# A hybrid attention and state-space layer: large loads on GpSimd's queue and later, combining weights a step later, the last gate loaded early, the output weight's split on GpSimd

## The chip, the cores and the metric

The kernel runs on one core of a Trainium2 chip. The metric is the device time of one execution in microseconds (us); the median of several executions is compared. A core has a matrix engine (TensorE, PE in the profile; PEld is its weight load), VectorE (DVE), ScalarE (ACT), GpSimd (POOL) and SyncE (SP), each with its own instruction stream that is worked off in order. DMA transfers are issued here by SyncE or by GpSimd.

## The reference

```python
proj = jnp.einsum('bsd,de->bse', x, w_in[layer])
q, k, v, z_att, z_ssm, xbc, dt_raw = jnp.split(proj, list(SPLITS), axis=-1)
o1, l1 = dilated_window_attention(q, k, v, slopes, 1)     # 16 heads of 64, window 128 steps
o2, l2 = dilated_window_attention(q, k, v, slopes, 4)
o3, l3 = dilated_window_attention(q, k, v, slopes, 16)
wts = jax.nn.softmax(jnp.stack([l1, l2, l3], axis=0), axis=0)
y_att = wts[0][..., None] * o1 + wts[1][..., None] * o2 + wts[2][..., None] * o3
y_att = rms_norm(y_att.reshape(Bsz, S, D_ATT) * jax.nn.silu(z_att), att_norm_g[layer])
xbc = jax.nn.silu(causal_depthwise_conv(xbc, conv_w[layer], conv_b[layer]))
...
y = ssd_chunked(xs_h, dt, a, bm, cm)                       # Mamba-2 scan, chunks of 128
y = y + d_skip[layer][:, None] * xs_h
y_ssm = rms_norm(y.reshape(Bsz, S, D_SSM) * jax.nn.silu(z_ssm), ssm_norm_g[layer])
mix = jnp.concatenate([y_att, y_ssm], axis=-1)
x = layer_norm(alpha * x + jnp.einsum('bse,ed->bsd', mix, w_out[layer]), ln_g[layer], ln_b[layer])
```

One sequence of 2048 positions, model width 1024, attention and state-space parts of 1024 columns each; all float32. The three outputs of a head are combined by a softmax over their log-sum-exps.

## The kernel before, in words

Matmul operands are split into a high and a low float32r part, and three products stand for one (high times high, high times low, low times high).

**Projections, convolution, scan (up to about 1270 us).** x is loaded transposed and split; v, then the convolution columns, then the state-space gate `z_ssm` (`ez`, L310), then q, k and the attention gate are projected, and the chunked scan (`ssd`) is woven between the last of these. Results go to DRAM tensors: d_qh, d_ql, d_kh, d_kl (high and low parts of q and k for each pair of heads), d_v (v in the block order of each of the three dilations), d_za (the attention gate), d_us (the state-space branch), d_uh (its first four row blocks, split already). In the z_ssm stage `split_w` also loads the output weight `wout` in halves of 512 columns (`woraw`), scales and rounds the high part (`wot`, L326), has VectorE form the low part (L327) and stores both to d_wo. In these stages a scheduler orders the instructions, on SyncE in the later ones too.

**Attention (about 1270 to 1830 us).** Here the order on TensorE, VectorE, ScalarE and GpSimd is that of the program. The list `todo` runs over 8 pairs of heads, 3 dilations d, 4 groups of blocks qd and 2 halves: a half-unit (d, qd, half) is two blocks of 128 queries for two heads. Step i of the loop does `scores` of half-unit i (matmuls S, L528; bias and row minimum on VectorE, L536; exponential on ScalarE, L544), `transposes` of half-unit i-2 (T, L557, evacuated by VectorE, L559) and `values` of half-unit i-3 (N, L577, into `num`). Most of the rest of the loop's body, including the places named (d, qd, half), goes by the half-unit whose `values` were just done. For each pair:

- `load_pair` and `load_qk` fetch the next pair's kh, kl, qh, ql (1 MB each, L462, GpSimd's queue), at (0,3,0); kh and kl have two buffers, qh and ql one.
- `load_dil` fetches a dilation's bias table `tb` and its v (1 MB, L472, SyncE's queue): for the next pair at (0,3,1) and (1,3,1), for dilation 2 of this pair at (0,3,1). v has three buffers.
- `permute` reorders qh and ql for dilations 1 and 2 into `qp` on GpSimd (L492, L496).
- `statistics` transposes the row minima and sums on TensorE (L595), copies them on ScalarE (L597, `sT`) and writes them to d_st with small SyncE DMAs (L599 to L605): after dilation 1, and after dilation 2 at the end of the pair. `gather` reads them back into `cm` in another layout (L611).
- `weights` of the pair before forms the softmax over dilations: part 0 (L618 to L621, VectorE and ScalarE) at (0,2,1), part 1 (L624 to L628, then the store to d_wd, L629) at (0,3,0).
- `combine` of the pair before, in four steps at (0,3,0), (1,0,0), (1,2,0), (2,2,0), on GpSimd: three times load the weights spread over partitions (`wb`, 1 MB, L642, SyncE), multiply `num` (L644) and add (L653); the fourth loads the gate (L657), multiplies (L659) and stores the branch to d_ua (L660).

In the last pair the loads of the output weight W from d_wo (`load_w`, L675, 1 MB each) and of d_uh (`fetch_parts`, L689) take the place of the next pair's loads, in buffers that have become free (`big`, `ring`).

**Output product (about 1830 us to the end).** For 16 blocks of 128 rows, `product` multiplies a branch (1 is state-space, 0 attention) by its half of W: 48 matmuls (L737 to L739) in two halves of 24, with a small matmul (L743) between the halves that sums the squares (`squares`, L712 and L714, on the branch's raw rows from `fetch_raw`) for the norm. `residual` loads x (L718); `add` applies the norm (L750, L755), `norm` is the layer norm. The branch 1 products of four row blocks come first, while pair 7 is finished: its gate is multiplied into `num` (L841, two on GpSimd, one on VectorE), then come `weights`, `combine` on VectorE, and the rest of W.

Of the kernel before, what the change touches and what calls it, by code (L numbers as in the profile page):

```python
# [9 lines left out]
F32 = mybir.dt.float32  # L10
# [8 lines left out]
NR = 16  # L19
# [9 lines left out]
def hybrid_layer(ctx, tc, xT, xc, w52, wv, convw, convb, dtb, alog, dskp, gcol, wout,  # L29
# [46 lines left out]
    with ExitStack() as c1:  # L76
# [178 lines left out]
        with tc.tile_pool(name="dtp", bufs=1, reuse_waits="tile") as dp, \  # L255
# [63 lines left out]
            def split_w(e):  # L319
                g = gc[:, e:e + 1]  # L320
                for hf in range(2):
                    s = slice(hf * 512, hf * 512 + 512)
                    raw = wo.tile([128, 512], F32, name="woraw")
                    nc.sync.dma_start(raw, wout[e * 128:(e + 1) * 128, s])
                    t = wo.tile([128, 2, 512], F32R, name="wot")
                    nc.scalar.activation(t[:, 0], raw, AF.Copy, scale=g)  # L326
                    nc.vector.scalar_tensor_tensor(t[:, 1], raw, g, t[:, 0].bitcast(F32), op0=OP.mult,  # L327
                                                   op1=OP.subtract)
                    nc.sync.dma_start(d_wo[e][:, :, s], t.bitcast(F32))
# [109 lines left out]
    with ExitStack() as c2:  # L439
# [11 lines left out]
        def load_pair(pr):  # L451

            A = {"pr": pr, "num": [], "tab": {}, "v": {}, "q": {0: []}, "k": []}
            load_qk(A, "k", d_kh, d_kl, qk[pr % 2])
            A["st"] = stp.tile([128, 192], F32, name="st")
            return A

        def load_qk(A, x, dh, dl, pool):
            to = A["q"][0] if x == "q" else A["k"]
            for src, n in ((dh, "h"), (dl, "l")):  # L460
                t = pool.tile([128, NR, NJ], F32R, name=x + n, bufs=1)
                nc.gpsimd.dma_start(f2(t), src[A["pr"]])  # L462
                to.append(t)

        def load_dil(A, d):

            pr = A["pr"]
            tb = A["tab"][d] = io.tile([128, 2, (128, 256, 256)[d]], F32, name=f"tb{d}", bufs=1)
            c0 = (512, 256, 0)[d]
            nc.sync.dma_start(tb, tabs[2 * pr:2 * pr + 2, :, c0:c0 + tb.shape[2]].rearrange("h p c -> p h c"))  # L470
            v = A["v"][d] = io.tile([128, 16, 128], F32, name="v", bufs=3)
            nc.sync.dma_start(v, d_v[d][:, :, pr * 128:pr * 128 + 128].rearrange("b p e -> p b e"))  # L472
# [219 lines left out]
        def fetch_raw(n, br):  # L692
            u = raw[n, br] = row().rearrange("p (c t) -> p c t", t=128)
            if br:
                for g in range(2):
                    nc.sync.dma_start(u[:, 4 * g:4 * g + 4], d_us[g][n])
            else:
                nc.sync.dma_start(u[:, 0:7], d_ua[n])
# [17 lines left out]
        def residual(n):  # L716
            o = O[n] = os_[n // 2][:, n % 2 * D:n % 2 * D + D] if n < 4 else O.pop(n - 4)
            nc.sync.dma_start(o, xc[n * 128:(n + 1) * 128, :])  # L718
# [3 lines left out]
        UT = ["num", "num", "num"]  # L722
# [56 lines left out]

        O = {}  # L780
# [5 lines left out]
        with tc.manual_schedule(engines={E.PE, E.DVE, E.Activation, E.Pool}):  # L786
            for i in range(len(todo) + TA + 1):
                if i < len(todo):
                    pr, d, qd, half = todo[i]
                    if i == 0:  # L790
                        pairs[0] = load_pair(0)
                        load_qk(pairs[0], "q", d_qh, d_ql, io)
# [11 lines left out]
                if i > TA:  # L804
# [4 lines left out]
                    if (d, qd, half) == (2, 3, 1):  # L809
                        statistics(pairs[pr], 1)  # L810
                        gather(pairs[pr])
                    if pr < 7:
                        if (d, qd, half) == (0, 3, 0):
                            pairs[pr + 1] = load_pair(pr + 1)
                            load_qk(pairs[pr + 1], "q", d_qh, d_ql, io)
                        if (qd, half) == (3, 1) and d < 2:
                            load_dil(pairs[pr + 1], d)
                    elif (d, qd, half) == (0, 3, 0):
                        for e, name in ((8, "kh_0"), (9, "kl_0"), (10, "qh"), (11, "ql")):
                            load_w(e, name)  # L820
                    elif (d, qd, half) == (1, 2, 0):
                        for e, name in ((12, "v"), (13, "qp"), (14, "qp")):
                            load_w(e, name)
                    elif (d, qd, half) == (1, 3, 1):
                        load_w(15, "v")
                    elif (d, qd, half) == (2, 1, 0):
                        for n in range(3):
                            fetch_parts(n, 1)
                    if pr and (d, qd, half) == (0, 3, 1):
                        load_dil(pairs[pr], 2)  # L830
                    if pr and d == 0 and (qd, half) in ((2, 1), (3, 0)):
                        weights(pairs[pr - 1], qd - 2)
                    step = ((0, 3, 0), (1, 0, 0), (1, 2, 0), (2, 2, 0))
                    if pr and (d, qd, half) in step:
                        combine(pairs[pr - 1], step.index((d, qd, half)))
            A = pairs[7]
            small = stp.tile([128, 192], F32, name="st")
            zt = cm_.tile([128, NR, NJ], F32, name="wb", bufs=3)
            nc.sync.dma_start(f2(zt), d_za[7])
            for d in range(3):  # L840
                (nc.vector if d == 2 else nc.gpsimd).tensor_tensor(A["num"][d], A["num"][d], zt, op=OP.mult)  # L841
            for n in range(3):
                fetch_raw(n, 1)
            os_ += [big("kh_1", F32), big("kl_1", F32)]
            for e, name in ((0, "qp"), (1, "qp"), (2, "v")):
                load_w(e, name)
            order = [(n, 1) for n in range(4)] + [(n, 0) for n in range(4)]
            order += [(n, br) for n in range(4, 16) for br in (1, 0)]
            squares(0, 1)
            residual(0)  # L850
            for i, (n, br) in enumerate(order):
                ps = product(n, br)
                if i == 0:
                    weights(A, 0)
                    residual(1)
                    weights(A, 1)
                if i == 1:
# [6 lines left out]
                    for e, name in ((3, "num"), (4, "num"), (5, "num"), (6, "wb"), (7, "wb")):  # L864
# [89 lines left out]
```

## Time and profile before

| | |
|---|---|
| median of 3 runs | 2244.34 us (2242.55 to 2248.68) |
| profiled execution | 2245.68 us, span 2243.9 us, mean TensorE clock 0.974 |
| busy | TensorE 2145.6 us, VectorE 1155.1, ScalarE 866.7, GpSimd 759.6 |
| DMA | 363.66 MB, 162 GB/s on the mean; SyncE's queue 306.76 MB, GpSimd's 54.53 MB |
| stage 1295 to 1835 us (attention) | TensorE busy 495.6 of 540 us, DMA share 0.68 |
| stage 1835 to 1900 us (first products) | TensorE busy 31.9 of 65 us, DMA share 0.89 |

How to read the lines. A row of the waits is: engine, tile and line that waited, the engine, tile and line that released it, us in total, times, longest. A row of the timeline is: start, duration, engine, line, operation, output and inputs, shape, count, and in brackets the idle time of that engine before it with what ended it. A row of a table by stretches is: the stretch, its length, then busy time and instructions of TensorE, its weight load, VectorE, ScalarE, GpSimd, then the granted clock, the DMA share and GB/s. A row of the chain of work that ended last is: start, duration, engine or DMA, tile.

### The profile page before, as it was taken

The numbers are of one execution on the slowest core, as the hardware profiler recorded it, in microseconds if no ns is written. First come the engines' busy times: TensorE is split into PE (matmuls) and PEld (weight loads), VectorE is DVE, ScalarE is ACT, GpSimd is POOL, SyncE is SP. The second block draws the span as 40 slices with busy tenths as digits, with TensorE's granted clock in tenths as the row PEclk, the third lists the DMA queues.
The fourth block names the chain that finished last, engine by engine and source line by source line (L and its number), as shares of the span: only waits on it lengthen the run. The fifth ranks groups of instructions, "written<-read, shape, count | busy, mean of one in ns | idle before, by whom it ended". The sixth has DMA issues, their size and how long they took to land.

```text
span 2243.9 us, 37059 instructions
## 1 busy us (share of the span) xinstructions
PE 2145.6 (96%) x13968; PEld 1789.4 (80%) x13968; DVE 1155.1 (51%) x2940; ACT 866.7 (39%) x2321; POOL 759.6 (34%) x527
## 2 busy tenths in 40 slices
PE   8999999999999999999999999899988976999998
PEld 8999888888778888888888788677776755888886
DVE  4000265553203555444644278777877756665655
ACT  4101122224322332232355378677776741222221
POOL 3101011010012555555654314456644562232322
PEclk9999999999999999999999889999999997999999
DMA  8544222226865565555543637767587698222220
GB/s 287 168 136 134 80 66 76 70 81 201 282 188 195 199 216 186 177 181 176 188 139 111 228 92 217 203 196 205 138 229 203 182 291 273 90 101 99 76 94 32
DMA packets 257219, 363.66 MB, mean 162 GB/s; under 512 B 37776, under 2 KB 175120, under 8 KB 246800
## 3 DMA queue, kind: packets, MB, share of 16 engines
q1 hardware_dynamic: 247952, 306.76, 44.9%
q0 software_dynamic: 9088, 54.53, 6.6%
q8 instruction: 110, 1.80, 0.3%
q14 instruction: 69, 0.57, 0.1%
HBM read 226.62 MB, written 134.61 MB: 161 GB/s over the span
## 4 chain that ended last, share of the span: by engine, by line
PE 80%; DMA 11%; DVE 3%; SPq 2%; issue 2%; ACT 2%; POOL 1%; ACTq 0%; DVEq 0%; POOLq 0%
PE pp L113 12%; PE pp L111 12%; PE pp L112 12%; PE S L528 6%; PE N L577 6%; PE T L557 6%; PE S L737 3%; PE S L739 3%; PE S L738 3%; DMA woraw<-wout 3%; DMA d_st<-sT 3%; PE pp L155 2%; PE pp L156 2%; PE pp L154 2%; PE T L737 2%
## 5 line engine op out<-in xcount | busy, mean ns | idle before, releaser
L111 PE MATMUL pp<-xh,whi 128*128 128x512 f32 x1408 | 550.8, 391 | 4.8 <-ACT ez L310 4.8
L112 PE MATMUL pp<-xl,whi 128*128 128x512 f32 x1408 | 549.5, 390 | 0.0
L113 PE MATMUL pp<-xh,wlo 128*128 128x512 f32 x1408 | 548.7, 390 | 0.0
L544 ACT ACTIVATE P<-P,st 128x256 f32<-128x256 f32 (+1 forms) x768 | 345.1, 451 | 97.2 <-DVE st L536 97.1
L111 PEld LDWEIGHTS pp<-xh,whi 128*128 128x128 f32 x1408 | 264.3, 188 | 61.1 <-ACT ez L310 6.7
L113 PEld LDWEIGHTS pp<-xh,wlo 128*128 128x128 f32 x1408 | 264.3, 188 | 55.1
L112 PEld LDWEIGHTS pp<-xl,whi 128*128 128x128 f32 x1408 | 264.4, 188 | 54.2
L536 DVE CUSTOM_DVE_ANT_0 P<-S,tb 128x256 f32<-128x256 f32 (+1 forms) x768 | 235.2, 362 | 105.8 <-PE S L528 48.6
L101 POOL TENSOR_TENSOR wlo<-wraw,whi 128x1024 fp32r<-128x1024 f32 x44 | 105.4, 2396 | 496.6 <-ACT whi L100 496.6
L577 PE MATMUL N<-PT,v 128*64 128x128 f32 x2400 | 179.4, 287 | 41.8 <-DVE PT L559 41.8
L559 DVE COPY PT<-T 128x512 f32<-128x512 f32 (+1 forms) x304 | 196.5, 677 | 2.3 <-PE T L557 2.2
L577 PEld LDWEIGHTS N<-PT,v 128*64 128x64 f32 x2400 | 131.3, 140 | 76.2 <-DVE PT L559 43.4
L557 PE MATMUL T<-ident,P 128*128 128x128 f32 x1200 | 180.0, 288 | 0.8 <-ACT P L544 0.3
L644 POOL TENSOR_TENSOR wb<-num,wb 128x2048 f32<-128x2048 f32 x21 | 96.2, 4580 | 171.3 <-DMA wb<-d_wd 101.2
L557 PEld LDWEIGHTS T<-ident,P 128*128 128x128 f32 x1200 | 131.7, 144 | 24.4 <-ACT P L544 1.8
L544 ACT ACTIVATION_READ_ACCUMULATOR P<-P,st 128x1 f32 x768 | 143.9, 187 | 0.0
L528 PE MATMUL S<-kh,qp 64*128 64x256 f32 (+1 forms) x1024 | 130.3, 313 | 0.0
L379 DVE TENSOR_SCALAR mt<-csb,cs 128x128 f32<-128x128 f32 x256 | 73.5, 357 | 74.3 <-DMA csb<-d_cs 66.1
L528 PEld LDWEIGHTS S<-kh,qp 64*128 64x128 f32 x1024 | 91.7, 194 | 23.0 <-issue 22.0
L154 PE MATMUL pp<-vh,xh 128*128 128x384 f32 (+1 forms) x304 | 95.1, 321 | 5.9 <-ACT xh L184 5.3
L128 DVE SCALAR_TENSOR_TENSOR ev<-pp,ev 128x512 f32<-128x512 f32 x64 | 44.0, 687 | 106.2 <-ACT ev L127 105.4
L714 DVE TENSOR_REDUCE tb<-P 128x128 f32<-128x1024 f32 x32 | 63.9, 1998 | 66.3 <-PE N L743 48.9
(288 smaller groups left out, 3737.9 us busy)
## 6 DMA issues: line engine op xcount, KB each, us to landing
v<-d_v SPq DMA_DIRECT2D x24, 1024.0 KB
wb<-d_wd SPq DMA_DIRECT2D x48, 512.0 KB
wraw<-w SPq DMA_DIRECT2D x44, 512.0 KB
d_wo<-wot SPq DMA_DIRECT2D x32, 512.0 KB
csb<-d_cs SPq DMA_DIRECT2D x32, 512.0 KB
d_v<-vt SPq DMA_DIRECT2D x64, 192.0 KB
d_za<-ev SPq DMA_DIRECT2D x32, 256.0 KB
d_xs<-cvo SPq DMA_DIRECT2D x8, 1024.0 KB
```

Of the source, the lines that this page charges most:

```text
L101: nc.gpsimd.tensor_tensor(lo, raw, hi.bitcast(F32), op=OP.subtract)
L111: nc.tensor.matmul(ps, hi[:, k, :], h, start=(k == 0), stop=False)
L112: nc.tensor.matmul(ps, hi[:, k, :], l, start=False, stop=False)
L113: nc.tensor.matmul(ps, lo[:, k, :], h, start=False, stop=(k == 7))
L154: nc.tensor.matmul(ps, h, vw[k][0], start=(k == 0), stop=False)
L528: nc.tensor.matmul(ov(sp[h][:, 256 * b:256 * b + w]), A["q"][d][x][hr, blk], kv(A["k"][y][hr]), start=(m == 0), stop=(m == 2))
L536: nc.vector.tensor_tensor_reduce(P[:, h, b, 256 - w:256], sp[h][:, c0:c0 + w], tab[:, h, tab.shape[2] - w:], 1.0, 3.0e38, OP.add, OP.min, ...
L544: nc.scalar.activation(p, p, AF.Exp, bias=stat(A, 0, d, h, blk), scale=-1.0, accum_out=stat(A, 1, d, h, blk))
L557: nc.tensor.transpose(tp[:, h, b], P[:, h, b, 128 * which:128 * which + 128], ident)
L559: nc.vector.tensor_copy(pt[:, :, bl[0]:2], tp[:, :, bl[0]:2])
L577: nc.tensor.matmul(nm[64 * h:64 * h + 64, bq * 128:bq * 128 + 128], v[:, k, 64 * h:64 * h + 64], pts[which][:, h, b], start=(f or not whic ...
L737: nc.tensor.matmul(ps, uh[:, e, :], wh, start=(e == 0), stop=False)
```

## The change

- `split_w`: the high part of the output weight is formed on GpSimd instead of ScalarE.
- `load_qk`: the next pair's four loads are issued together, in the order qh, kh, ql, kl, at (1,0,0), behind `combine` step 0; before, kh, kl, qh, ql at (0,3,0).
- `load_dil`: v is issued on GpSimd's queue, in program order; `tb` stays on SyncE.
- `weights` parts 0 and 1 go to (0,3,0) and (0,3,1); `combine` steps to (1,0,0), (1,1,0), (1,3,0), (2,2,0), and both now stand ahead of the loads in the loop's body.
- Last pair: W 8 to 12 at (1,0,0) behind `combine`, the gate z7 at (1,1,0) on GpSimd's queue, W 13 and 14, `fetch_parts`(0) and one gate multiplication on GpSimd at (1,3,0), W 15 at (1,3,1), `fetch_parts`(1) at (2,2,0). The other two gates are done on VectorE behind `weights` of pair 7.
- Behind the loop: `squares` comes right after the first raw rows; raw rows 0 and 1 and residuals 0 and 1 are loaded by GpSimd's queue; all of W 0 to 7 is loaded after pair 7's `combine`, in other buffers.

```diff
-                    nc.scalar.activation(t[:, 0], raw, AF.Copy, scale=g)
+                    nc.gpsimd.tensor_scalar(t[:, 0], raw, g, None, op0=OP.mult)
...
-            load_qk(A, "k", d_kh, d_kl, qk[pr % 2])
...
-        def load_qk(A, x, dh, dl, pool):
-            to = A["q"][0] if x == "q" else A["k"]
-            for src, n in ((dh, "h"), (dl, "l")):
-                t = pool.tile([128, NR, NJ], F32R, name=x + n, bufs=1)
-                nc.gpsimd.dma_start(f2(t), src[A["pr"]])
+        def load_qk(A):
+            pr = A["pr"]
+            for x, src, to in (("qh", d_qh, A["q"][0]), ("kh", d_kh, A["k"]),
+                               ("ql", d_ql, A["q"][0]), ("kl", d_kl, A["k"])):
+                t = (io if x[0] == "q" else qk[pr % 2]).tile([128, NR, NJ], F32R, name=x, bufs=1)
+                nc.gpsimd.dma_start(f2(t), src[pr])
                 to.append(t)
...
-            nc.sync.dma_start(v, d_v[d][:, :, pr * 128:pr * 128 + 128].rearrange("b p e -> p b e"))
+            nc.gpsimd.dma_start(v, d_v[d][:, :, pr * 128:pr * 128 + 128].rearrange("b p e -> p b e"))
...
-                    nc.sync.dma_start(u[:, 4 * g:4 * g + 4], d_us[g][n])
+                    (nc.gpsimd if n < 2 else nc.sync).dma_start(u[:, 4 * g:4 * g + 4], d_us[g][n])
...
-            nc.sync.dma_start(o, xc[n * 128:(n + 1) * 128, :])
+            (nc.gpsimd if n < 2 else nc.sync).dma_start(o, xc[n * 128:(n + 1) * 128, :])
...
-        UT = ["num", "num", "num"]
+        UT = ["num", "num", "qp"]
...
+        def gate(d, eng):
+            num = f2(pairs[7]["num"][d])
+            eng.tensor_tensor(num, num, zt7, op=OP.mult)
...
+                    at = d, qd, half
+                    if pr and at in ((0, 3, 0), (0, 3, 1)):
+                        weights(pairs[pr - 1], half)
+                    step = ((1, 0, 0), (1, 1, 0), (1, 3, 0), (2, 2, 0))
+                    if pr and at in step:
+                        combine(pairs[pr - 1], step.index(at))
                     if pr < 7:
-                        if (d, qd, half) == (0, 3, 0):
+                        if at == (0, 3, 1):
                             pairs[pr + 1] = load_pair(pr + 1)
-                            load_qk(pairs[pr + 1], "q", d_qh, d_ql, io)
+                        if at == (1, 0, 0):
+                            load_qk(pairs[pr + 1])
                         if (qd, half) == (3, 1) and d < 2:
                             load_dil(pairs[pr + 1], d)
-                    elif (d, qd, half) == (0, 3, 0):
-                        for e, name in ((8, "kh_0"), (9, "kl_0"), (10, "qh"), (11, "ql")):
+                    elif at == (1, 0, 0):
+                        for e, name in ((8, "kh_0"), (9, "kl_0"), (10, "qh"), (11, "ql"), (12, "v")):
                             load_w(e, name)
-                    elif (d, qd, half) == (1, 2, 0):
-                        for e, name in ((12, "v"), (13, "qp"), (14, "qp")):
+                    elif at == (1, 1, 0):
+                        zt7 = big("num", F32)
+                        nc.gpsimd.dma_start(zt7, d_za[7])
+                    elif at == (1, 3, 0):
+                        for e, name in ((13, "qp"), (14, "qp")):
                             load_w(e, name)
-                    elif (d, qd, half) == (1, 3, 1):
+                        fetch_parts(0, 1)
+                        gate(0, nc.gpsimd)
+                    elif at == (1, 3, 1):
                         load_w(15, "v")
-                    elif (d, qd, half) == (2, 1, 0):
-                        for n in range(3):
-                            fetch_parts(n, 1)
+                    elif at == (2, 2, 0):
+                        fetch_parts(1, 1)
...
-                    if pr and d == 0 and (qd, half) in ((2, 1), (3, 0)):
-                        weights(pairs[pr - 1], qd - 2)
-                    step = ((0, 3, 0), (1, 0, 0), (1, 2, 0), (2, 2, 0))
-                    if pr and (d, qd, half) in step:
-                        combine(pairs[pr - 1], step.index((d, qd, half)))
...
-            zt = cm_.tile([128, NR, NJ], F32, name="wb", bufs=3)
-            nc.sync.dma_start(f2(zt), d_za[7])
-            for d in range(3):
-                (nc.vector if d == 2 else nc.gpsimd).tensor_tensor(A["num"][d], A["num"][d], zt, op=OP.mult)
-            for n in range(3):
-                fetch_raw(n, 1)
             os_ += [big("kh_1", F32), big("kl_1", F32)]
-            for e, name in ((0, "qp"), (1, "qp"), (2, "v")):
-                load_w(e, name)
+            fetch_raw(0, 1)
+            squares(0, 1)
+            residual(0)
+            fetch_raw(1, 1)
+            residual(1)
+            fetch_parts(2, 1)
+            fetch_raw(2, 1)
...
-            squares(0, 1)
-            residual(0)
             for i, (n, br) in enumerate(order):
                 ps = product(n, br)
                 if i == 0:
                     weights(A, 0)
-                    residual(1)
                     weights(A, 1)
+                    gate(1, nc.vector)
+                    gate(2, nc.vector)
...
-                    for e, name in ((3, "num"), (4, "num"), (5, "num"), (6, "wb"), (7, "wb")):
+                    for e, name in enumerate(("num", "num", "num", "num", "qp", "v", "wb", "wb")):
                         load_w(e, name)
```

More of the change, by code (lines that the diff above doesn't have):

```diff
@@ L791, in hybrid_layer @@
                         pairs[0] = load_pair(0)
-                        load_qk(pairs[0], "q", d_qh, d_ql, io)
+                        load_qk(pairs[0])
                         for k in range(3):
@@ L825, in hybrid_layer @@
                         load_w(15, "v")
-                    elif (d, qd, half) == (2, 1, 0):
-                        for n in range(3):
-                            fetch_parts(n, 1)
-                    if pr and (d, qd, half) == (0, 3, 1):
+                    elif at == (2, 2, 0):
+                        fetch_parts(1, 1)
+                    if pr and at == (0, 3, 1):
                         load_dil(pairs[pr], 2)
-                    if pr and d == 0 and (qd, half) in ((2, 1), (3, 0)):
-                        weights(pairs[pr - 1], qd - 2)
```

## The prediction

> **What bounds the kernel now.** The page's first section comes first, then the waits in total, since they say what little TensorE loses.
>
> ```profile
> PE 2145.6 (96%) x13968; PEld 1789.4 (80%) x13968; DVE 1155.1 (51%) x2940; ACT 866.7 (39%) x2321; POOL 759.6 (34%) x527
> ```
> ```profile
> PE N L577 <- DVE PT L559: 41.8, 7, 9.0
> PE N L743 <- DVE tb L714: 33.1, 2, 17.6
> ```
> ```profile
> PE pp L111 <- ACT ez L310: 4.8, 4, 1.7
> PE S L737 <- DMA num<-d_uh: 2.3, 2, 1.3
> ```
> TensorE is busy 96%, and no edit removes a matmul. All that can be won is idle time: 2243.9 - 2145.6 = 98.3 us, and 41.8 + 33.1 + 4.8 + 2.3 = 82.0 us of it lies at places that the diff touches. Each place is read by itself.
>
> First the attention stage. The waits, and then the timeline of VectorE at two successive pairs of heads:
>
> ```profile
> DVE mm L618 <- DMA cm<-d_st: 45.8, 6, 9.8
> ```
> ```profile
> 1362.57 0.18 DVE L618 TENSOR_TENSOR mm<-cm 128x32 f32<-128x32 f32 x1
> 1364.63 0.25 DVE L624 TENSOR_TENSOR cm<-cm 128x96 f32<-128x96 f32 x1
> 1434.40 0.19 DVE L618 TENSOR_TENSOR mm<-cm 128x32 f32<-128x32 f32 x1 [9.79 <-DMA cm<-d_st]
> ```
> L618 opens `weights`. VectorE works in program order, so while it waits there for `cm`, the score and transpose evacuations behind it wait too, and TensorE stands still at L577. A pair without the wait takes 1434.40 - 9.79 - 1362.57 = 62.0 us; with it 71.8 (1362.57 to 1434.40). Why is `cm` late? SyncE's and GpSimd's issues, first where VectorE did not wait, then where it did:
>
> ```profile
> 1351.16 3.30 SPq L605 DMA_DIRECT2D d_st<-sT  x4
> 1356.97 0.38 SPq L611 DMA_DIRECT2D cm<-d_st  x1
> ```
> ```profile
> 1411.08 0.37 SPq L660 DMA_DIRECT2D d_ua<-wb  x1
> 1412.00 0.69 SPq L472 DMA_DIRECT2D v<-d_v  x1
> 1413.13 5.37 SPq L605 DMA_DIRECT2D d_st<-sT  x4
> 1432.22 0.38 SPq L611 DMA_DIRECT2D cm<-d_st  x1
> ```
> ```profile
> 1415.45 0.59 POOL L462 DMA_DIRECT2D kh<-d_kh  x1
> 1421.39 0.53 POOL L462 DMA_DIRECT2D qh<-d_qh  x1 [4.81 <-PE T L557]
> ```
> ```profile
> 1420.00:1424.00 4.00, 4.00 (x52) 3.16 (x48) 3.10 (x21) 3.70 (x18) 1.05 (x2) 1.00 1.14 426
> ```
> The gather of `cm` is issued once the statistics have landed: 5.8 us after their first issue on quiet queues (1351.16 to 1356.97), 19.1 us when d_ua, v, kh, kl, qh and ql, 1 MB each, are in flight (1413.13 to 1432.22; kl and ql follow kh and qh at once; the last columns of the window are clock, DMA share, 1.14, and GB/s, 426).
>
> Next the output product, by the timeline:
>
> ```profile
> 1829.22 0.30 PE L595 MATMUL N<-ident,st 128*64 128x128 f32 x1
> 1830.78 11.22 SPq L839 DMA_DIRECT2D wb<-d_za  x1
> 1849.36 2.29 DVE L841 TENSOR_TENSOR num<-num,wb 128x2048 f32<-128x2048 f32 x1 [21.08 <-DMA wb<-d_za]
> 1853.47 2.62 DVE L618 TENSOR_TENSOR mm<-cm 128x32 f32<-128x32 f32 x1
> 1853.53 0.58 PE L743 MATMUL N<-one,tb 128*128 128x1 f32 x2 [15.56 <-DVE tb L714]
> 1856.13 4.50 DVE L619 TENSOR_TENSOR mm<-mm,cm 128x32 f32<-128x32 f32 x1
> 1862.70 9.25 DMA d_wd<-cm
> 1875.05 15.37 DMA wb<-d_wd
> 1897.17 0.58 PE L743 MATMUL N<-one,tb 128*128 128x1 f32 x2 [17.56 <-DVE tb L714]
> ```
> Two stalls. The first product's norm waits for `squares`, which stands on VectorE behind the gate L841, which waits for a `d_za` load whose issue alone took 11.22 us. The third product's norm waits behind pair 7's `combine`: weights, d_wd, three wb loads. From the end of attention (1829.5, the last transposition) to the second release it is 67.6 us.
>
> **The change, part by part.** I call T the issue of the weights (d_wd) of a pair; 1437.91 below.
>
> *Dilation weights later.* Part 0 goes from (0,2,1) to (0,3,0), part 1 from (0,3,0) to (0,3,1): one half-unit each in this code, 1362.57 to 1364.63, 2.06 us. Alone that takes 6 x 2.06 = 12.4 us off the 45.8. The rest must come from an earlier `cm`.
>
> *Loads moved.* q and k of the next pair are now issued at (1,0,0) behind `combine` 0, hence after T; v goes from SyncE to GpSimd. Neither is beside the statistics then, but for v of dilation 1 and d_ua, 2 MB where there were 6. The new need stands about 11.5 + 2.06 = 13.5 us after the first d_st issue (1413.13 to 1424.61, plus the shift). Quiet chain: 5.8 us, and 2.2 for the gather (1432.22 to 1434.40) = 8.0; 2 MB at some 400 GB/s add 5, together 13. So I take the 45.8 as gone. What is late next is kl. Rows behind T, the landing times and two TensorE units:
>
> ```profile
> 1437.91 0.36 SPq L629 DMA_DIRECT2D d_wd<-cm  x1
> 1450.33 9.17 POOL L644 TENSOR_TENSOR wb<-num,wb 128x2048 f32<-128x2048 f32 x2 [27.88 <-DMA wb<-d_wd]
> ```
> ```profile
> kl<-d_kl POOLq DMA_DIRECT2D x8, 1024.0 KB, 9.4
> ql<-d_ql POOLq DMA_DIRECT2D x8, 1024.0 KB, 8.9
> ```
> ```profile
> 1444.31 1.09 PE L557 MATMUL T<-ident,P 128*128 128x128 f32 x8
> 1447.25 1.09 PE L557 MATMUL T<-ident,P 128*128 128x128 f32 x8
> ```
> `combine` 0 starts T + 12.4 and takes 4.6, so the four loads are issued from T + 17. Four such loads took about 9.4 + 8.9 = 18.3 us in two lots: kl lands at T + 35. Its scores come 13 half-units of 2.94 us behind T: T + 38. That is cover of 3 us; gone, each us costs 6 us over six pairs. Three wb and the second v share the engines, so I charge 2 of the 45.8 us: -44.
>
> *v on GpSimd's queue.* It waits there for TensorE's values of the unit just done, and `combine`, the permutes and q/k are queued behind it. Its issue on that queue has no row. Nearest:
>
> ```profile
> L689 POOL DMA_DIRECT2D num<-d_uh x8: 696/705/715, 1821.6 to 1862.9; - x8
> ```
> That load has 256 contiguous runs, kh's has 128 at 0.53 us, v has 2048 (128 partitions x 16 runs of 512 B). By the slope (0.70 - 0.53)/128 = 1.3 ns a run, v is 3.0 us; by proportion, 0.70 x 8 = 5.6; without any dependence on runs 0.53. I take 3.0, on the slope of the two rows. GpSimd's chain in a pair is then v, v (hidden in the 12.4 us wait), 12.4 + 4.6 + 2.2 (q/k) + 9.2 + 4.6 (permute) + 9.2 + 3.0 + 4.6 + 4.6 = 54.4 us of 62.0: hidden. SyncE is rid of three 1 MB loads.
>
> The Trainium skill, "SBUF — State Buffer", section "SBUF: two separate sides", says a DMA issued from GpSimd starves while VectorE runs a two-port operation, since GpSimd can't write descriptors. It gives about 620 ns alone and 3100 ns beside such a copy; by that fivefold, v would be an estimated 15 us and the kernel slower. The qh row shows 0.53 us with VectorE busy 3.1 of the 4 us around it, so the trace does not show that price here.
>
> *Last gate early, tail loads.* zt7 loads at (1,1,0), one gate runs on GpSimd at (1,3,0) (4.6 us), two on VectorE behind the weights (2 x 2.29). `squares`(0) no longer stands behind it, and L618/L619, 2.62 and 4.50 us beside GpSimd's gate against 0.19 above, get back some 6.7 us. But GpSimd now issues W 8 to 12 only behind `combine` 0 (T + 17), and its order is c1, zt7, c2, W13/14, uh0, gate, W15, c3, uh1: 17 + 2.8 + 9.2 + 0.6 + 9.2 + 1.1 + 1.4 + 4.6 + 0.5 + 4.6 + 1.4 = T + 52, where raw(0) is issued at last. Attention ends at T + 40.5 (1785.78 to 1829.22 below is 43.4 in the old order, less one half-unit). Some 6.5 MB stand before raw(0) from T + 38.5; at 400 GB/s it lands at T + 55 to 58. Rows for this part: the last T, d_uh's landing, the reduction of `squares`, and two matmuls of a product.
>
> ```profile
> 1785.78 0.36 SPq L629 DMA_DIRECT2D d_wd<-cm  x1
> ```
> ```profile
> DMA to landing us min/median/max: 9.2/13.8/19.4
> ```
> ```profile
> 1851.57 1.91 DVE tb L714
> ```
> ```profile
> 1837.10 0.40 PE L737 MATMUL S<-v,num 128*128 128x512 f32 x1
> 1837.34 0.39 PE L738 MATMUL S<-v,num 128*128 128x512 f32 x1
> ```
> `squares` (ACT's part taken as 1, VectorE 1.9) ends at T + 61. First stall: the product starts at about T + 45, when uh0 has landed, reaches the norm 24 matmuls x 0.235 = 5.6 us later and waits 10. Then VectorE: weights to T + 65, gates and squares(1) to T + 71, while d_wd's 9.25 (to T + 74) and the wb loads' 15.37 run (to T + 90), `combine`'s end and squares(2): T + 97, or 56.5 us behind attention's end where it was 67.6. That is -11. On quiet queues (the statistics in 8 us, d_wd in 5) it is about T + 89: -19. I take -15; bounds -8 (raw(0) lands 13.8 us behind its issue, as d_uh's loads did) and -33 (both stalls gone).
>
> The eight W loads of the attention half now all stand behind `combine` 7: the last six MB from about T + 90, at 400 GB/s to T + 105, needed from T + 108 on: +1 (0 to 5).
>
> *Weight splitting on GpSimd.*
>
> ```profile
> 505.00:690.00 185.00, 180.25 (x791) 147.48 (x790) 40.63 (x63) 60.07 (x88) 20.17 (x9) 1.00 0.70 217
> ```
> The 32 ACT operations that leave stood before `ez`, waiting for `woraw`; behind `ez` lie the 4.8 us at L111. GpSimd, busy 20.2 of 185 us (fifth column of times), has room; what it could delay is `wlo`, one per projection of some 23 us, split a projection ahead. -4 (0 to -4.8).
>
> *Start of attention.* Pair 0's three v issues now precede its permutes on GpSimd: 9 us, against eight half-units of some 2 us before dilation 1's scores need them. 0 (+2).
>
> **Sum**, against the profiled run's 2245.7 us: -44 - 15 + 1 - 4 = -62, 2183.7. That run is 1.3 us above the median of 2244.3, so 2182.
>
> **Rivals.**
> *The loads still collide (A).* kl lands after T + 38, or d_ua, if SyncE's order has it before d_st, holds the statistics until GpSimd's c3 (T + 50). For it: 3 us of cover; against: the 9.4 and 8.9 were themselves taken on full queues. kl 5 us beyond its cover in six pairs is 30 us: 2212. The Trainium skill, "DMA: Bandwidth & Descriptors", section "Issuing engines are not separate DMA queues", says that all issuers' DMAs run on the same 16 engines and interleave. By it the queue alone buys nothing; the 1.14 share above agrees. If no time of the loads helped either, attention would win the 12.4 us alone: 2214.
> *The tail wins nothing (B).* raw(0) behind GpSimd's list; 2182 + 15 = 2197.
> *Slower (C): GpSimd becomes the bound.* Its chain with an issue price V for v is 12.4 + 39 + V, or 39 + 3V once 2V exceeds 12.4. From V = 7.7 us a pair is longer than 62; six pairs eat the 62 us from 3V + 39 = 72.3, V = 11.1 us. At V = 15: 6 x 22 = 132 less 62, 2314; at 12, 2260. Against: 5.6 us is the most that rows allow.
> *Nothing moves (D)*: if SyncE's statistics stay late through something unseen and the tail too: 2240.
>
> **Numbers.** The forecast 0.50 (its own range 2165 to 2200), A 0.24, B 0.12, C 0.06, D 0.03, better than forecast 0.05 (attention -47, tail -33, split -4.8: 2158). Range 2158 to 2218: from the better case past both versions of A, without C, D and A's worst. Within 0.3%, about 7 us, is what a measurement here can't tell from no change: faster 0.91, same 0.03 (D), slower 0.06 (C).
>
> **What would show it.** Right: no VectorE wait at L618 inside attention, pairs 62 us apart at L618, cm's gather within 10 us of d_st; v issues of about 3 us on GpSimd; one stall of about 10 at each of the two L743, with the second release 48 to 57 us behind attention's end; L111 without ACT waits. Wrong: TensorE waiting at L528 for kl (A), GpSimd without idle time in attention (C), L577 waits left (A, D).

## The result, and the profile after

The changed kernel takes 2187.99 us (median of 4 runs, 2186.43 to 2193.83) where the kernel before took 2243.45 on the same chip: a ratio of 0.976 (95% interval 0.9727 to 0.9793). The forecast was 2182, in a range of 2158 to 2218. A second comparison gave 2189.07 against 2241.58, 0.9772 (0.9758 to 0.9786). The profiled execution of after has a span of 2192.0 us (before 2243.9).

Busy time, and what TensorE and VectorE wait for in the kernel after:

```profile
PE 2138.5 (98%) x13968; PEld 1784.6 (81%) x13968; DVE 1166.2 (53%) x2941; ACT 847.8 (39%) x2289; POOL 838.8 (38%) x589
```
```profile
PE N L743 <- DVE tb L714: 23.7, 2, 19.2
PE S L737 <- DMA num<-d_uh: 7.0, 1, 7.0
PE T L557 <- DVE PT L559: 5.9, 8, 0.8
```
```profile
DVE mm L618 <- DMA cm<-d_st: 5.1, 1, 5.1
```

The 41.8 us at L577 and the 4.8 us at L111 are gone; of the 45.8 us at L618 one wait of 5.1 is left, in the output product. The two L743 waits are still there, 23.7 us where they were 33.1, and a wait of 7.0 us for d_uh has joined them.

To see where the time went, cut the span at three places: the first and the last transposition of statistics (L595), and the second release of the norm (L743). The first cut pair comes from these rows of the instructions at L595, before and then after (the last two times are the starts of the first and the last):

```profile
L595 PE MATMUL N<-ident,st x16: 298/314/329, 1326.9 to 1829.2; 128*128 128x128 f32 x8, 128*64 128x128 f32 x8
```
```profile
L595 PE MATMUL N<-ident,st x16: 298/313/329, 1321.5 to 1779.5; 128*128 128x128 f32 x8, 128*64 128x128 f32 x8
```

All profiled executions, cut that way (us; e1 to e12 are the experiments below):

| kernel | up to the first L595 | attention: first to last L595 | tail: to the second release | rest |
|---|---|---|---|---|
| before | 1326.9 | 502.3 | 68.0 | 346.7 |
| after | 1321.5 | 458.0 | 65.7 | 346.8 |
| after, second profile (e12) | 1322.2 | 457.9 | 59.8 | 347.0 |
| e1: before, weights and combine later | 1329.3 | 502.3 | 71.0 | 346.8 |
| e9: e1, k and q loads later | 1328.2 | 457.8 | 71.9 | 347.2 |
| e2: after, weights as before | 1321.6 | 457.8 | 62.3 | 347.2 |
| e3: after, k and q loads as before | 1325.7 | 495.0 | 63.4 | 347.4 |
| e4: after, v on SyncE | 1322.2 | 458.1 | 64.7 | 347.2 |
| e5: after, split on ScalarE | 1323.3 | 457.9 | 61.5 | 347.6 |
| e6: after, W behind wb | 1322.4 | 458.5 | 55.4 | 346.9 |
| e7: after, W 8 and 9 early | 1322.6 | 458.0 | 65.5 | 345.9 |
| e8: e6 and e7 | 1321.8 | 458.1 | 57.1 | 346.6 |
| e10: e6, loads behind the gather | 1325.4 | 458.4 | 56.9 | 346.8 |
| e11: e10, residuals behind the weights | 1322.1 | 458.4 | 56.9 | 346.6 |

So after wins 5.4 us up to the attention, 44.3 in it, 2.3 in the tail (8.2 in the second profile) and nothing in the rest: 51.9 of 51.9. The attention's length repeats within 0.7 us wherever it is short; the first cut (1321.5 to 1325.7 with the changed split) and the tail repeat only within 4 to 6 us, so small differences there show nothing.

The attention's 44.3 us, in the view by windows of this stretch, before and then after (columns: length, busy time of TensorE, its weight loads, VectorE, ScalarE and GpSimd, granted clock, DMA share, GB/s):

```profile
1326.90:1829.20 502.30, 460.22 (x5423) 376.50 (x5421) 392.15 (x1722) 371.22 (x1498) 269.53 (x184) 0.95 0.69 196
```
```profile
1321.50:1779.50 458.00, 452.06 (x5424) 368.94 (x5422) 391.74 (x1722) 372.62 (x1498) 290.68 (x200) 1.00 0.72 212
```

Only 41.8 + 0.3 - 5.9 = 36.2 us of it are waits (L577 and L557). The other 8.2 us are TensorE's own busy time, 460.2 to 452.1 for the same matmuls: without the stalls the granted clock is 1.00 instead of 0.95. Here a stall cost more than its wait.

A pair of heads after, SyncE's and then GpSimd's timeline, v's issues, and kl's landing:

```profile
1408.34 2.18 SPq L605 DMA_DIRECT2D d_st<-sT  x4
1414.47 0.38 SPq L611 DMA_DIRECT2D cm<-d_st  x1
1414.90 0.54 SPq L660 DMA_DIRECT2D d_ua<-wb  x1
1425.77 0.36 SPq L629 DMA_DIRECT2D d_wd<-cm  x1
```
```profile
1437.92 4.57 POOL L644 TENSOR_TENSOR wb<-num,wb 128x2048 f32<-128x2048 f32 x1 [13.05 <-DMA wb<-d_wd]
1442.42 0.60 POOL L462 DMA_DIRECT2D qh<-d_qh  x1
1444.08 0.57 POOL L462 DMA_DIRECT2D kl<-d_kl  x1
```
```profile
L472 POOL DMA_DIRECT2D v<-d_v x24: 1151/1198/1242, 1244.6 to 1730.2; - x24
kl<-d_kl POOLq DMA_DIRECT2D x6, 1024.0 KB, 15.6
```

The gather of `cm` is issued 6.1 us behind the statistics (19.1 before), with one v of 1 MB beside them; in the six pairs it is 5.0 to 7.0 us. The 19.1 is not every pair of before. It is 18.2 to 19.1 us in the three pairs where SyncE issues d_ua ahead of the statistics, and 10.4 to 11.7 in the three where d_ua comes behind the gather:

```profile
1485.23 2.82 SPq L605 DMA_DIRECT2D d_st<-sT  x4
1495.62 0.38 SPq L611 DMA_DIRECT2D cm<-d_st  x1
1496.10 0.53 SPq L660 DMA_DIRECT2D d_ua<-wb  x1
```

The loads of q and k are issued 17 to 18 us behind d_wd, and kl lands 15.6 us after its issue (the median of six).

The tail after, from its chain of waits, and TensorE's waits in the timeline:

```profile
1781.75 11.66 DMA d_st<-sT
1793.49 11.46 DMA cm<-d_st
1807.45 3.21 DMA d_wd<-cm
1814.25 24.14 DMA wb<-d_wd
```
```profile
1786.74 0.79 PE L737 MATMUL S<-kh,num 128*128 128x512 f32 x1 [6.96 <-DMA num<-d_uh]
1799.93 0.59 PE L743 MATMUL N<-one,tb 128*128 128x1 f32 x2 [4.53 <-DVE tb L714]
1845.15 0.58 PE L743 MATMUL N<-one,tb 128*128 128x1 f32 x2 [19.20 <-DVE tb L714]
```

The first stall fell from 15.56 to 4.53 us, and the gates that held VectorE are gone; but the statistics now take 11.66 and 11.46 us, and wb 24.14 where it took 15.37. Most of what was won ahead of them was given back there.

### The profile page after: what moved, and what is told of

Same layout as the page of the kernel before. It is cut to its first block, busy times and chain, and to the rows that moved or that the text cites. A ratio compares the mean times of both kernels' runs of the same rounds, so it can differ in the third digit from the quotient of the medians.

```text
span 2192.0 us, 37071 instructions
## 1 busy us (share of the span) xinstructions
PE 2138.5 (98%) x13968; PEld 1784.6 (81%) x13968; DVE 1166.2 (53%) x2941; ACT 847.8 (39%) x2289; POOL 838.8 (38%) x589
## 3 DMA queue, kind: packets, MB, share of 16 engines
q1 hardware_dynamic: 197408, 278.45, 41.8%
## 4 chain that ended last, share of the span: by engine, by line
PE 89%; DMA 4%; DVE 4%; ACT 2%; SPq 1%; issue 1%; POOL 0%; DVEq 0%; POOLq 0%; ACTq 0%
PE pp L112 14%; PE pp L111 14%; PE pp L113 14%; PE N L577 6%; PE T L557 6%; PE S L528 6%; PE S L737 3%; PE S L739 3%; PE S L738 3%; PE pp L155 2%; PE pp L156 2%; PE pp L154 2%; PE T L737 2%; PE T L738 2%; PE T L739 2%; PE ss L386 1%
## 5 line engine op out<-in xcount | busy, mean ns | idle before, releaser
L111 PE MATMUL pp<-xh,whi 128*128 128x512 f32 x1408 | 550.3, 391 | 0.0
L113 PEld LDWEIGHTS pp<-xh,wlo 128*128 128x128 f32 x1408 | 264.3, 188 | 55.4
L111 PEld LDWEIGHTS pp<-xh,whi 128*128 128x128 f32 x1408 | 264.4, 188 | 54.7
L557 PE MATMUL T<-ident,P 128*128 128x128 f32 x1200 | 179.4, 286 | 6.3 <-DVE PT L559 5.9
L577 PE MATMUL N<-PT,v 128*64 128x128 f32 x2400 | 176.4, 284 | 0.0
L577 PEld LDWEIGHTS N<-PT,v 128*64 128x64 f32 x2400 | 129.2, 138 | 33.2 <-issue 22.6
L557 PEld LDWEIGHTS T<-ident,P 128*128 128x128 f32 x1200 | 129.7, 142 | 31.5 <-DVE PT L559 7.3
L100 ACT CAST whi<-wraw 128x1024 fp32r<-128x1024 f32 x44 | 46.1, 1047 | 138.3 <-PE pp L112 130.5
```

The lines of the kernel that those rows point to most:

```text
L111: nc.tensor.matmul(ps, hi[:, k, :], h, start=(k == 0), stop=False)
L113: nc.tensor.matmul(ps, lo[:, k, :], h, start=False, stop=(k == 7))
L557: nc.tensor.transpose(tp[:, h, b], P[:, h, b, 128 * which:128 * which + 128], ident)
L577: nc.tensor.matmul(nm[64 * h:64 * h + 64, bq * 128:bq * 128 + 128], v[:, k, 64 * h:64 * h + 64], pts[which][:, h, b], start=(f or not whic ...
```

## The experiments

**e1: the later places of weights and combine alone, in the kernel before.**

```diff
-if pr and d == 0 and (qd, half) in ((2, 1), (3, 0)):
-    weights(pairs[pr - 1], qd - 2)
-step = ((0, 3, 0), (1, 0, 0), (1, 2, 0), (2, 2, 0))
+if pr and d == 0 and qd == 3:
+    weights(pairs[pr - 1], half)
+step = ((1, 0, 0), (1, 1, 0), (1, 3, 0), (2, 2, 0))
```

> The kernel before, with only the places of `weights` and `combine` of the change; all loads, the tail and the weight split stay as before. If the moment of the loads decides, the later place takes 2.06 us off each of six waits at L618, 12.4 us in all: about 2231 us, with some 33 us of wait left at L618. If the later place is what removed the waits, they are gone here too: about 2198 us.

Measured: 2245.34 us against 2242.78, ratio 1.0022 (1.0005 to 1.0038). Nothing is won, and the attention is as long as before to the tenth, 502.3 us. Waits at L577 and its stretch by windows:

```profile
PE N L577 <- DVE PT L559: 36.9, 6, 8.8
```
```profile
1329.30:1831.60 502.30, 464.25 (x5423) 380.20 (x5421) 392.59 (x1722) 372.90 (x1498) 269.86 (x184) 0.95 0.70 196
```

4.1 us of wait did go (38.0 against 42.1, with L557's), but TensorE's busy time rose by 4.0; why is open. VectorE's waits at L618 shrank by 7.0 us, to 38.8. With the four loads still beside them the statistics are about as slow as before: the gather comes 10.3 to 19.5 us behind them in the six pairs.

**e2: the changed kernel with the weights at their old places.** Edit: `at in ((0, 2, 1), (0, 3, 0))` with part `at[1] - 2`.

> The changed kernel with `weights` back at (0,2,1) and (0,3,0), `combine` and all loads as changed. If the moment of the loads decides, `cm` is there some 5 us before its new need, so the old place 2.06 us earlier costs nothing: 2188 us within 5, no wait at L618 inside attention. If the later place was needed, the waits return: 2200 us or more.

Measured: 2191.60 us, ratio 0.9777 (0.9755 to 0.9799), attention 457.8 us. Two waits at L618, 3.8 us together, are back inside the attention and cost it nothing. By e1 and e2 the later weights are neither enough nor needed.

**e3: the changed kernel with the k and q loads as before.**

```diff
-for x, src, to in (("qh", ...), ("kh", ...), ("ql", ...), ("kl", ...)):
+for x, src, to in (("kh", ...), ("kl", ...), ("qh", ...), ("ql", ...)):
...
-if at == (0, 3, 1):
+if at == (0, 3, 0):
     pairs[pr + 1] = load_pair(pr + 1)
-if at == (1, 0, 0):
     load_qk(pairs[pr + 1])
```

> The changed kernel with the next pair's k and q loads back at (0,3,0) in the old order kh, kl, qh, ql; v stays on GpSimd's queue, weights stay late. If the moment of these four loads decides, the gather of `cm` again comes 10 to 19 us behind the first statistics store where 13.5 are covered: waits of 3 to 6 us in each of six pairs, 2205 to 2225 us. If v's queue was what mattered: 2188 us.

Measured: 2229.51 us against 2242.78, ratio 0.9948 (0.9932 to 0.9964). The attention is 495.0 us long: of 44 us, 37 are lost again. They are lost in fewer and longer waits than before:

```profile
PE N L577 <- DVE PT L559: 34.7, 2, 20.8
```
```profile
1572.24 0.19 DVE L618 TENSOR_TENSOR mm<-cm 128x32 f32<-128x32 f32 x1 [21.13 <-DMA cm<-d_st]
```

They do not come about as in the kernel before. SyncE's timeline ahead of the longer one:

```profile
1537.61 0.32 SPq L605 DMA_DIRECT2D d_st<-sT  x1
1549.31 0.37 SPq L660 DMA_DIRECT2D d_ua<-wb  x1
1549.72 3.80 SPq L605 DMA_DIRECT2D d_st<-sT  x3
1555.10 0.38 SPq L611 DMA_DIRECT2D cm<-d_st  x1
```

In SyncE's order d_ua stands ahead of three of the four stores of statistics, and waits for GpSimd's last multiplication (L659, which ends at 1549.28): the second version of rival A. Then k, q and two v are issued between 1553.7 and 1558.2, beside the gather, and L618 starts only 17.1 us behind its issue. At the other wait it is the same: d_ua ahead of all four stores, and 16.3 us from the gather to L618 (1696.04 to 1712.3). In the other pairs the gather comes 3 to 8 us behind the statistics, and VectorE does not wait. So e3 shows that the moment of the four loads matters, but by a late start and a slow gather, not by slow statistics.

**e9: the moment of the k and q loads alone (with e1's places), in the kernel before.** Edit to e1: the four loads at (1,0,0) behind combine, in the order qh, kh, ql, kl.

> The kernel before with two parts of the change alone: the weights and combine places, and the next pair's k and q loads behind the first combine in the order qh, kh, ql, kl. v stays on SyncE, and the kernel before's split and tail stay. Theory T1 (the moment of the k and q loads carries the attention's gain): cm is issued about 6 to 7 us after d_st, L618 <- DMA cm under 10 us in all, L577 under 5, L743 <- DVE tb near 33; the attention wins about 46 and nothing else is won, so 2243.4 - 46 = 2197 us (2192 to 2206). Rival T2 (it takes v on GpSimd's queue or the last pair's new places as well): cm again 12 us or more after d_st, L618 over 20 us, 2212 to 2235 us. The first run with the weights and combine places alone gave 2245.

Measured: 2208.75 us (2194.28 to 2213.28) against 2242.47, ratio 0.9834 (0.9797 to 0.987). The attention is 457.8 us, all of the change's gain, with no wait at L618. SyncE's timeline of a pair:

```profile
1413.89 0.37 SPq L472 DMA_DIRECT2D v<-d_v  x1
1415.02 2.44 SPq L605 DMA_DIRECT2D d_st<-sT  x4
1417.56 0.40 SPq L660 DMA_DIRECT2D d_ua<-wb  x1
1420.29 0.38 SPq L611 DMA_DIRECT2D cm<-d_st  x1
```

v (1 MB) goes ahead of the statistics and d_ua (1 MB) between them and the gather, and the gather still comes 5.3 us behind them (5.3 to 6.8 in the six pairs). With the four loads of k and q beside them too, in e1, it was 10.3 to 19.5. Apart from their order among themselves, the moment of these loads is all that e9 changes in e1, so this is the cleanest test of the cause. e9 still ends above its expected 2197: in its profile the tail is 71.9 us long where before's is 68.0, with a wait of 8.1 us for d_uh, and the first cut comes 1.3 us later. Tails of the same code differ by as much, and e9's own runs spread from 2194 to 2213, so whether the later places cost in the tail isn't shown.

**e4: the changed kernel with v on SyncE.** Edit: `nc.sync.dma_start(v, ...)`.

> The changed kernel with v's loads back on SyncE's queue, all else as changed. If the moment of the k and q loads decides, little changes: 2188 to 2195 us, v in packets of 512 B. If the queue of v decides (SyncE blocked before the statistics, or the engines held by small packets), the waits at L618 return: 2200 us or more.

Measured: 2191.63 us, ratio 0.9768 (0.9736 to 0.98); attention 458.1 us. v's queue is worth nothing that shows here. The Trainium skill, "DMA: Bandwidth & Descriptors", section "Issuing engines are not separate DMA queues", says as much: all issuers' transfers run on the same 16 engines. The runs agree, 458.1 us on the one queue and 458.0 on the other.

**e5: the changed kernel with the split on ScalarE.** Edit: `nc.scalar.activation(t[:, 0], raw, AF.Copy, scale=g)`.

> The changed kernel with the output weight's high part back on ScalarE. By the sum, 3.5 to 4.8 us longer than the changed kernel, 2192 us, with the 4.8 us of wait at L111 for ez back; if the earlier start of attention (3.4 us) had another cause: 2188 us and attention starting as early.

Measured: 2196.42 us (2192.22 to 2198.09), ratio 0.9798 (0.9778 to 0.9818). The wait at L111 for `ez` is back, 3.9 us in 4 waits. By the medians the part is worth 7 to 8 us, by the profile's first cut 1.8 (1323.3 against 1321.5), which is within the spread of that cut. The interval overlaps that of the changed kernel, so the size isn't settled.

**e6: W 0 to 7 so ordered that the first waits for a wb buffer**, so that none is issued before wb has landed.

```diff
-for e, name in enumerate(("num", "num", "num", "num", "qp", "v", "wb", "wb")):
+for e, name in ((6, "wb"), (0, "num"), (1, "num"), (2, "num"), (3, "num"), (4, "qp"), (5, "v"), (7, "wb")):
```

> The changed kernel with the last loads of W in another order: W 6 first, whose wb buffer is free only after combine's second step, so that no W load runs beside pair 7's first two weight loads. If W 0 to 2 beside the three wb loads made these take 24 us instead of 15, the second release at L743 comes 6 to 9 us earlier: 2179 to 2182 us. If the spread loads are slow by themselves (220 to 240 GB/s in both kernels), it comes no earlier: 2188 us, or up to 5 us more because W 0 to 7 land later.

Measured: 2186.02 us, ratio 0.9753 (0.9736 to 0.9771). In its chain wb takes 15.5 us, not 24.14, and the tail is 55.4 us long:

```profile
1813.97 15.54 DMA wb<-d_wd
```

Three W loads of 1 MB beside wb had made it slow: in the seven profiles with these loads there it takes 19.3 to 24.1 us, in e6, e8 and e10 15.0 to 15.5. The rest of the kernel stays at 346.9 us, so W isn't late for being issued later. By the medians e6 is only 2 to 3 us below the changed kernel's two, and the intervals overlap.

**e7: W 8 and 9 early**, at (0,2,0), so that less stands on GpSimd's queue near the end of the attention.

> The changed kernel with W 8 and 9 loaded at (0,2,0) of the last pair, ahead of pair 6's weights, instead of at (1,0,0): 2 MB less in the queues when attention ends. If the backlog there makes the statistics and the gather slow (11.7 and 11.5 us), the first product starts 3 to 5 us earlier and weights of pair 7 some 5 us earlier: 2181 to 2185 us. If the raw and residual loads behind attention make the backlog: 2187 us. If 2 MB beside pair 6's gather make it late: 2190 us with a wait at L618 at the last pair's start.

Measured: 2193.56 us, ratio 0.9788 (0.977 to 0.9806): no gain, the wait for d_uh is 8.5 us.

**e8: e6 and e7 together.**

> Both tail edits together (W 8 and 9 at (0,2,0), W 6 first among the last loads). If both gains are there and apart: 2172 to 2178 us, faster than the changed kernel; if one of the theories is wrong, the better single edit's time.

Measured: 2185.95 us, ratio 0.9755 (0.9733 to 0.9776), as e6 alone.

**e10: e6 with the loads of the first products behind the gather.** GpSimd issues the last pair's gather, and behind it raw(0), residual(0), uh1, raw(1), residual(1), uh2.

```diff
-nc.sync.dma_start(cm, dap(d_st[A["pr"]], ...))
+(nc.gpsimd if A["pr"] == 7 else nc.sync).dma_start(cm, dap(d_st[A["pr"]], ...))
```

> The changed kernel with the last eight weight loads in the order of e6, and the last pair's gather (cm) issued by GpSimd ahead of raw(0), raw(1), both residuals, uh1 and uh2, so that those loads, 3.5 MB, are issued only when d_st has landed. Theory T1 (those loads beside the statistics make d_st and cm take 23 us where the kernel before had about 10): from d_st's issue to cm's landing 8 to 14 us, second release of product 1's N (L743) at about 44 to 52 us after the attention's end instead of 55 in e6, while the first N and uh1 come about 5 us later; 2178 to 2183 us. Rival T2 (the same bytes then stand beside d_wd and wb, or the first product waits for raw(0) and uh1 what the second release wins): wb over 20 us or waits at L737 and the first L743 of 15 us and more together, 2185 to 2190 us. Rival T3 (d_st is slow for W13 to W15 and uh0, which are issued ahead and stay): d_st still over 9 us, 2184 to 2187 us.

Measured: 2185.68 us, ratio 0.9737 (0.9721 to 0.9753). The gather is issued 10 us behind d_st and lands 3.7 us later, about 14 us for the two instead of 23: the loads did make the statistics slow. But ScalarE, in program order, had residual(1) to scale before the exp of the weights:

```profile
1799.80 8.32 DMA kh<-xc
1809.11 0.28 ACT cm L621
```

**e11: e10 with both residuals behind the weights.**

> e10 with residual(0) and residual(1) issued, and scaled on ScalarE, behind the weights of the last pair. In e10 the exp of the weights (L621) stood behind the scaling of residual(1), which waited for its load: cm was there about 1799 us of the span, L621 ran at 1809.1. Theory T1 (the order on ScalarE took back what the earlier cm won): L621 about 14 to 18 us after the attention's end instead of 25, second release of N (L743) about 48 to 52 us after it instead of 57; 2177 to 2182 us. Rival T2 (another of the loads is then late: the residuals, now behind, hold the first add, or wb is over 20 us): 2184 to 2189 us.

Measured beside e12: 2184.90 us (2182.66 to 2185.73), ratio 0.9747 (0.9733 to 0.9761). The exp now runs at 1800.1, 19.6 us behind the attention's end where it was 25.3 in e10, and the second release comes no sooner, 56.9 us as in e10. Its chain shows where the gain went:

```profile
1801.85 7.01 DMA d_wd<-cm
1812.11 18.49 DMA wb<-d_wd
```

d_wd took 2.12 us and wb 15.54 in e6. The two residual loads, issued at 1800.7, now stand beside d_wd; what slowed wb isn't shown. The time is the one of rival T2, though its sign, wb over 20 us, did not appear. e11 is the fastest version run, 4.2 us below the changed kernel measured beside it.

**e12: the changed kernel once more**, beside e11.

> The changed kernel once more, unchanged, beside the last version, to tell the two apart on one chip: 2186 to 2191 us, ratio to the kernel before 0.974 to 0.978. By the profiles e6 should be 7 to 8 us faster than this; by the medians of different calls it is 2.

Measured: 2189.07 us (2188.68 to 2191.97), ratio 0.9772 (0.9758 to 0.9786); its runs and e11's do not overlap. Its tail took 59.8 us where the first profile had 65.7. In the six profiles of this same tail code (after, e2 to e5, e12) it takes 59.8 to 65.7, 62.9 on the mean, so its gain on the 68.0 of before (a single profile) is some 5 us, not the 2.3 that one profile shows.

## Why the prediction was right, and where its steps failed

**Attention, -44 forecast, -44.3 measured.** The cause is the one named, large loads beside the small statistics: e9 wins all of it with the moment of the k and q loads (e1, the same without that, wins nothing). e3 takes 37 us of it back, but by way of SyncE's order and the gather. How much d_ua ahead of the statistics added in half of before's pairs was not tested by itself. Within it three things were otherwise.

The step "alone that takes 6 x 2.06 = 12.4 us off the 45.8" fell: in e1 only 7.0 us of VectorE's wait went and the attention won 0, and e2 lost nothing. Why the later step did not pay one for one is open.

"2 MB at some 400 GB/s add 5" was hardly there either: 5.0 to 7.0 us from statistics to gather after, with v beside them, and 5.3 to 6.8 in e9, with v ahead of them and d_ua right behind, against 5.8 on quiet queues.

And that the 44 came out so near is luck, by errors that cancel. TensorE's waits there were 41.8, not the 45.8 that VectorE waited, and small waits at L557 grew by 5.6; the sum was made up by 8.2 us of faster matmuls, which no term had.

**The steps behind d_wd** came out near: combine 0 starts at T + 12.15 (12.4), the q and k loads follow at T + 17, kl lands at T + 34 (35). No wait of TensorE for kl is among its waits, so rival A's first version did not occur; d_ua stands behind the gather in this order, so its second did not either (in e3 it did).

**v's issue** takes 1.2 us, not 3.0: no more than a sixth of the 7.7 us from which rival C would have counted. By the slope it would have been 1.3 ns a run; the 2048 runs do not cost that. The Trainium skill, "SBUF — State Buffer", section "SBUF: two separate sides", was the source of an estimate of 15 us; the longest of 24 issues is 1.242 us, so the trace shows no such starving here.

**Split, -4 forecast:** the waits at L111 are gone (4.8 us), and e5 brings 3.9 of them back. **Start of attention, 0:** the first cut comes 5.4 us earlier, 4.7 in e12; with the spread of that cut a loss or gain of 2 us can't be told. **W 0 to 7, +1:** the rest is 0.1 to 0.3 us longer.

**Tail, -15 forecast, -2.3 and -8.2 in two profiles.** This is the term that was mis-sized, and from it comes that the forecast is 6 to 7 us too low. Its first half held: raw(0) was issued at T + 49 (T + 52), and the first release came at T + 61.5 (T + 61). Its second half, "weights to T + 65" and "the wb loads' 15.37", took the transfers at the length they had in the kernel before. There GpSimd was held by the gates until 1860.5 us: 237 GB/s passed beside the statistics (1843 to 1853.5), and beside wb came two loads of W, at 1881.7 and 1887.8. The change takes that hold away. Then 385 GB/s pass in the 20 us from 1780, 7.7 MB, beside the statistics (96 KB), and W 0 to 2 beside wb: the weights end at T + 69 and the second release comes at T + 106.7 instead of T + 97 (T is 1738.39 here). Against the sum the weights are 4 us later and wb takes 8.8 us more and starts some 4 us later behind d_wd; d_wd, 9.25 us in the sum, took only 3.21. The view of the DMA engines from 1776 to 1850 of after, in 40 slices, shows it (tenths of busy share, then GB/s):

```profile
DMA  9999999999999993095999999999999999528999
GB/s 436 407 405 375 385 433 353 341 354 377 407 413 404 394 347 116 12 223 106 331 204 230 213 226 226 213 252 230 213 208 275 244 253 410 195 35 283 412 412 321
```

The engines are busy nearly throughout, and while wb is spread over the partitions they move 204 to 275 GB/s instead of 400. The tail by windows, from the end of the attention to the second release, for before, after, e6 and e11:

```profile
1829.50:1897.00 67.50, 32.24 (x125) 25.05 (x124) 29.55 (x23) 11.29 (x15) 17.73 (x13) 0.78 0.91 279
```
```profile
1780.00:1845.00 65.00, 34.68 (x124) 27.23 (x124) 24.95 (x24) 11.29 (x15) 17.81 (x23) 0.76 1.02 277
```
```profile
1781.00:1836.00 55.00, 32.59 (x125) 25.30 (x124) 24.78 (x24) 11.66 (x15) 18.13 (x23) 0.81 1.00 292
```
```profile
1781.00:1837.00 56.00, 32.86 (x124) 25.91 (x124) 24.72 (x24) 11.18 (x15) 18.72 (x24) 0.80 1.03 290
```

Length times rate gives 18.8 MB before, 18.0 after, 16.1 in e6 and 16.2 in e11. In the three kernels after the change the share is 1.00 and more on the mean. e6 put some 2 MB behind the release and won 4 to 10 us of tail against the two profiles of after; e10 and e11 put the same bytes as e6 in another order and won nothing. That is rival B in part, for another reason than the one given: raw(0) was in time. That bytes alone set the length is not shown: the six profiles of after's tail code move 18.2 to 18.5 MB in 59.8 to 65.7 us. Why these differ is open; wb was 24.14 us in after and 19.33 in e12.

A third stall adds to it. Behind each of the three waits shown above matmuls are slow for a while (see the last section); the sum of what they lose is 8.5 us, against 4.7 us behind the two long waits of before. So of the 4.7 us by which the waits shrank (23.7 + 7.0 against 33.1 + 2.3), 3.8 went back into a slower clock.

**The signs.** Of those named for right, pairs 62 us apart at L618 (62.5), the gather within 10 us, no wait at L618 inside the attention and none for ScalarE at L111 came. Three did not: v's issues of 3 us, stalls of about 10 us at each L743 (4.53 and 19.20), and the second release 48 to 57 us behind the attention's end (65.7 and 59.8). The range's lower end of 2158 is also 1.5 us below its own terms (2244.3 - 47 - 33 - 4.8 = 2159.5), which changes nothing.

## What to carry to other kernels

A small transfer on the critical path is priced by what stands beside it: ask of each large load at what moment it is issued; on which queue made no difference here (e4). Ask of each issue, too, what stands ahead of it in its engine's order and waits (e3). Where the DMA engines were already busy nearly throughout, another order only moved the wait (e10, e11); moving bytes behind the release shortened it (e6). When an edit frees an engine that also issues loads, read the old trace for what that engine's idle time had been keeping apart.

## What the runs showed of the hardware that had not been expected

TensorE's clock after a stall. In the timeline after, matmuls of the same shape stand 0.43 us apart behind the 4.53 us wait, up to 6.1 us from the release, and 0.23 us apart from there on:

```profile
1805.65 0.63 PE L737 MATMUL S<-v,num 128*128 128x512 f32 x1
1806.07 0.63 PE L738 MATMUL S<-v,num 128*128 128x512 f32 x1
1806.50 0.43 PE L739 MATMUL S<-v,num 128*128 128x512 f32 x1
1806.77 0.40 PE L737 MATMUL S<-qp,num 128*128 128x512 f32 x1
1807.00 0.40 PE L738 MATMUL S<-qp,num 128*128 128x512 f32 x1
```

Behind each of the waits of 4.53, 6.96 and 19.20 us 13 to 15 matmuls lose 0.19 us each and more, 2.7 to 3.0 us; behind the two long waits of the kernel before it was 15 and 8 matmuls, and behind its waits of 1.0 and 1.3 us the spacing is 0.23 at once. In e5 slow matmuls follow a wait of 3.68 us. The Trainium skill, "TensorE: Matmul & The Clock Gate", section "Part 1: The HAM clock gate", has TensorE fall to half clock after an idle window of about 3.4 us and rise again after a busy one, in windows that run on freely. The trace agrees: the threshold lies between 1.3 and 3.7 us here, and the slow stretches last 3.4 us (8 matmuls) to 6.4 us (15), one window to two.

GpSimd issues a load of 2048 runs of 512 B in 1.2 us, against 0.53 us for one of 128 runs of 8 KB: 0.35 ns a run between these two. The load of d_uh, 256 runs, takes 0.70 us and is not on that line, so the number of runs alone does not give the price.
